# Causal masks added by VectorE instead of TensorE in a sparse-attention block, and ten early down-projection chunks instead of six

## The chip, the cores and the metric

The kernel runs on one core of a Trainium2 chip. The metric is the device time of one execution in microseconds (us), the median of several runs; lower is better. The core has five engines that run their own instruction queues in order: TensorE (PE; its weight loads are listed as PEld), VectorE (DVE), ScalarE (ACT), GpSimd (POOL) and SyncE (SP), which issues the DMAs. Matrix products are accumulated in PSUM; everything else on chip lies in SBUF.

## The reference

One decoder layer on x of 1024 tokens by 1024 channels, float32. RMSNorm and an input projection feed three groups of heads: pooling, native sparse attention and a short gated convolution. Their outputs go through w_out and are added to x; then comes a gated FFN of width 2816. The part that the change touches is the sparse attention, with 8 heads in 2 groups of 64 channels. Each head has three branches: compressed keys, selected blocks ("slc") and a sliding window of 512 ("win"). Cut to the two branches with full keys:

```
s_s = q . k_slc * scale - slope * d_s          # keys of the selected blocks
s_s = where(d_s >= 0, s_s, -1e30);  p_s = softmax(s_s);  o_s = p_s @ v_slc

ok  = (d_w >= 0) & (d_w < WINDOW)              # d = query position - key position
s_w = q . k_win * scale - slope * d_w
p_w = softmax(where(ok, s_w, -1e30));  o_w = p_w @ v_win

o = gate0 * o_cmp + gate1 * o_slc + gate2 * o_win
...
x = x + W_down( silu(causal_dwconv3(W_a h2)) * (W_b h2) )
```

## The kernel before

**Tiling.** Tokens are cut into 8 tiles of 128 queries. Products of float32 accuracy are made from a high and a low part of each operand (`split`, L86 to L89: ScalarE makes the high part, VectorE or GpSimd the low one), so one product is three matrix products. The program is written in the Tile framework: a planner decides, before the kernel runs, the order of the instructions on each engine, and puts in the semaphores. The order on an engine is then fixed.

**Attention.** `attend` (L639) walks over the tiles; for each it takes 2 groups and 2 branches (1 is the window, 0 the selected blocks), and weaves the scores of one unit (`scores`, L560) with the values of the unit before (`values`, L593). A row is one head of one unit: 128 queries against `ns` key tiles. `span` gives ns: the window branch takes at most 5 tiles of keys, the selected branch i + 1. With up to 4 key tiles a row is one chunk of columns, above that two. For each chunk, two products go to the PSUM tile S: L572 (the query's parts against the high key parts) and L573 (the query's high part, the slopes' rows and, for i >= 4, the selection's penalty, against the low key parts). The causal mask is added by a third product, L578, of a bfloat16 identity with `m_diag` (zeros and -2^100), into the last 128 columns of the row; in the window branch of tiles 4 to 7, L576 adds `m_edge` in the same way to the first 128 columns. Then VectorE takes the negative maximum of the row (L580), ScalarE the exp and its sum (L583), VectorE the reciprocal (L586), and GpSimd scales the row by it and the gate (L588). `values` transposes the row on TensorE (L97), splits it (`put_pt`, L472) and multiplies it with the values (L609, L610).

**Two attention stages.** Tiles 0 to 3 run first (L668), with two score buffers of one PSUM bank; the planner lays the convolution and pooling products beside them. Tiles 4 to 7 run second (L802), with one score buffer of two banks. Beside them lie the projection of the first four tiles (`project`), all 22 `up` products of the FFN for the first half of the tokens (their results go to DRAM as `hid0`), and then the early chunks.

**Early chunks.** The loop at L911 takes the first `EARLY` = 6 of 22 chunks of the down projection, two at a time, for tiles 0 to 3: it loads the hidden values (`hidden_in`, L874) and the down weights (`down_in`, L880), splits them, and adds the products (L925) to x2 on VectorE (L926). The memory of x2 is that of the up products' input, so this loop starts behind the last of these.

**FFN.** After the attention, `hidden_a` and `hidden_b` (L941, L950) go over the pairs of chunks in the order of `todo` (L980): first those that were not early, for which `down` (L955) also makes the products of tiles 0 to 3 (`first_half`, L983; two pairs ahead, the rest one per turn of the loop at L991), then the early ones, for which only tiles 4 to 7 are left. The down weights of every chunk are loaded and split here, also those of the early ones.

Of the kernel before, what the change touches and what calls it, by code (L numbers as in the profile page):

```python
# [10 lines left out]
BF16 = mybir.dt.bfloat16  # L11
I32 = mybir.dt.int32
AF = mybir.ActivationFunctionType
ALU = mybir.AluOpType
AX = mybir.AxisListType
# [3 lines left out]
P = 128  # L19
T = 1024  # L20
# [2 lines left out]
KT = D // P  # L23
DFF = 2816
NCH = DFF // P
EARLY = 6
DH = 64
EPS = 1e-6
NEG = -(2.0 ** 100)
# [16 lines left out]
def kernel(  # L46
# [7 lines left out]
    pe, dve, act, pool = nc.tensor, nc.vector, nc.scalar, nc.gpsimd  # L54
# [8 lines left out]
    cst = ctx.enter_context(tc.tile_pool(name="cst", bufs=1))  # L63
# [6 lines left out]
    def nm(s):  # L70
        uid[0] += 1
        return f"{s}_{uid[0]}"
# [242 lines left out]
    for s in range(2):  # L315
# [10 lines left out]
        bias = small(1, "cbias", 64)  # L326
# [34 lines left out]
    for c in range(2):  # L361
        wq = load_w(C_Q + 256 * c, (pool, dve))
        for i in range(NT):
# [6 lines left out]

    ident_b = cst.tile([P, P], BF16, name="ident_b")
    dve.tensor_copy(ident_b, ident)
    m_diag = cst.tile([P, P], BF16, name="m_diag")
    pool.memset(m_diag, 0.0)
    pool.affine_select(m_diag, m_diag, pattern=[[-1, P]], base=0, channel_multiplier=1,
                       compare_op=ALU.is_ge, fill=NEG)
    m_edge = cst.tile([P, P], BF16, name="m_edge")
    pool.memset(m_edge, 0.0)
    pool.affine_select(m_edge, m_edge, pattern=[[1, P]], base=-1, channel_multiplier=-1,
                       compare_op=ALU.is_ge, fill=NEG)  # L380
    m_cmp = cst.tile([P, NT, 64], BF16, name="m_cmp")
    pool.memset(m_cmp, 0.0)
    pool.affine_select(m_cmp, m_cmp, pattern=[[P, NT], [-16, 64]], base=-31, channel_multiplier=1,
# [94 lines left out]
        return hi, lo  # L478

    qAs, pcs, yfs, pos = {}, {}, {}, {}  # L480
    new_s, new_p = [None], [None]

    def prepare(i):

# [75 lines left out]
    def scores(i, g, br, pbs):  # L560

        s0, ns = span(i, br)
        nck = 1 if ns <= 4 else 2
        cw = ns * P // nck
        krows = 112 if (br == 0 and i >= 4) else 66
        for hh in range(4):
            S = new_s[0]()
            for c in range(nck):
                cols = slice(s0 * P + c * cw, s0 * P + (c + 1) * cw)
                last = c == nck - 1  # L570
                edge = br == 1 and i >= 4 and c == 0
                pe.matmul(S[:, c, :cw], qAs[i, g][:, hh, :], kA[br, g][:, cols], start=True, stop=False)  # L572
                pe.matmul(S[:, c, :cw], qB[g][i % QBUF][0:krows, hh, :], kB[br, g][0:krows, cols],  # L573
                          start=False, stop=not (last or edge))
                if edge:
                    pe.matmul(S[:, c, 0:P], ident_b, m_edge, start=False, stop=not last)  # L576
                if last:
                    pe.matmul(S[:, c, cw - P : cw], ident_b, m_diag, start=False, stop=True)  # L578
            mx = small(1, "mx1")
            dve.tensor_reduce(mx, S[:, 0:nck, :cw], axis=AX.XY, op=ALU.max, negate=True)  # L580
            pb = new_p[0](br)
            sw = small(1, "sw1")
            act.activation(pb[:, : ns * P].rearrange("p (c n) -> p c n", c=nck), S[:, 0:nck, :cw],  # L583
                           AF.Exp, bias=mx, accum_out=sw)
            rc = small(1, "rc1")
            dve.reciprocal(rc, sw)  # L586
            col = 8 * (2 if br == 1 else 1) + 4 * g + hh
            pool.tensor_scalar(pb[:, : ns * P], pb[:, : ns * P], rc, gat[:, i, col : col + 1],  # L588
                               ALU.mult, ALU.mult)
            pbs.append(pb)  # L590
            yield
# [203 lines left out]

    def f2k(dt=F32):
        return f2.tile([P, 512], dt, tag="f2k", bufs=5, name=nm("f2k"))

    sth = ExitStack()
    h2p = sth.enter_context(tc.tile_pool(name="h2a", bufs=1, side="right"))  # L800
# [224 lines left out]
```

## Time and profile before

| what | value |
|---|---|
| median of 3 runs | 1352.73 us (1352.63 to 1353.0) |
| profiled execution | 1353.7 us |
| its span, first to last instruction | 1351.9 us |
| mean granted TensorE clock | 0.995 |
| TensorE busy | 1313.2 us (97%) |
| VectorE busy | 765.6 us (57%) |
| ScalarE busy | 535.8 us (40%) |
| GpSimd busy | 495.1 us (37%) |

The profile is of one execution. The span is what the trace covers; the time of the execution is 1.8 us more. "Busy" counts an instruction from its start to its end; matrix products overlap in the array, so their listed duration is longer than the distance between two starts. Where a cost on TensorE is wanted, the distance between starts is to be read.

### The profile page before, as it was taken

The page shows a single profiled execution, that of the slowest core. Times are in us where ns is not written, and L with a number is a line of the kernel's source. Part 1 is how long each engine was busy: PE and PEld are TensorE (multiplying, and loading weights), DVE is VectorE, ACT ScalarE, POOL GpSimd, SP SyncE. Part 2 cuts the span into 40 slices and gives each one's busy share as a digit, 9 for nine tenths or more (in the row PEclk, how much of TensorE's full clock was granted, in tenths as well). Part 3 has the DMA queues.
Part 4 walks back from the last instruction along what each step waited for, and adds up shares of the span by engine and source line. Part 5 has one row for each costly group of instructions (what it writes and reads, how often), then busy time and mean ns, then how long its engine had stood idle before and what let it go on. Part 6 is the DMA issues. An engine that isn't in the chain of part 4 may idle for free. (4 is left out here: it accounts for less than half of the span.)

```text
span 1351.9 us, 17751 instructions
## 1 busy us (share of the span) xinstructions
PE 1313.2 (97%) x6670; PEld 1081.1 (80%) x6670; DVE 765.6 (57%) x1351; ACT 535.8 (40%) x972; POOL 495.1 (37%) x447
## 2 busy tenths in 40 slices
PE   6999999999998999999999999999999999999998
PEld 5999987678776788888888887778888788888886
DVE  6772556666776446445745667774454555454554
ACT  5441444444465444444544445453312322132220
POOL 3453723331334344434443545253313331242220
PEclk9999999999998999999999999999999999999999
DMA  9011320226342233222222273132222422243221
GB/s 274 16 48 56 102 58 20 86 97 220 125 149 94 78 101 94 86 79 86 87 78 78 86 251 100 48 110 71 84 62 78 125 63 78 79 156 92 84 74 62
DMA packets 142498, 128.93 MB, mean 95 GB/s; under 512 B 10595, under 2 KB 119373, under 8 KB 142413
## 3 DMA queue, kind: packets, MB, share of 16 engines
q1 hardware_dynamic: 142269, 127.71, 30.5%
q8 instruction: 52, 0.85, 0.3%
q14 instruction: 33, 0.27, 0.1%
q10 hardware_dynamic: 144, 0.10, 0.0%
HBM read 105.50 MB, written 22.28 MB: 95 GB/s over the span
## 5 line engine op out<-in xcount | busy, mean ns | idle before, releaser
L89 POOL TENSOR_TENSOR wlo<-wst,whi 128x1024 fp32r<-128x1024 f32 x109 | 264.3, 2438 | 281.5 <-ACT whi L88 273.6
L588 POOL TENSOR_SCALAR pb<-pb,rc,gat 128x640 f32<-128x640 f32 (+7 forms) x128 | 106.0, 829 | 317.8 <-DVE rc L586 302.0
L88 ACT ACTIVATE whi<-wst 128x1024 fp32r<-128x1024 f32 x124 | 127.1, 1056 | 125.7 <-DMA wst<-in_ffn_up_dram 80.1
L972 DVE TENSOR_TENSOR x<-dn,x 128x1024 f32<-128x1024 f32 x72 | 87.9, 1221 | 104.0 <-PE dn L969 104.0
L852 PE MATMUL fill<-h2a_hi,wlo 128*128 128x512 f32 x352 | 141.4, 402 | 0.0
L850 PE MATMUL fill<-h2a_hi,whi 128*128 128x512 f32 x352 | 141.3, 401 | 0.0
L851 PE MATMUL fill<-h2a_lo,whi 128*128 128x512 f32 x352 | 141.3, 401 | 0.0
L583 ACT ACTIVATE pb<-S,mx 128x640 f32<-128x640 f32 (+7 forms) x128 | 89.5, 700 | 114.6 <-DVE mx L580 108.4
L580 DVE TENSOR_REDUCE mx<-S 128x1 f32<-128x640 f32 (+7 forms) x128 | 89.6, 702 | 69.2 <-PE S L578 68.7
L477 DVE TENSOR_TENSOR ptl<-tr,pth 128x512 fp32r<-128x512 f32 x140 | 94.3, 685 | 54.7 <-PE acc L610 29.7
L476 ACT ACTIVATE pth<-tr 128x512 fp32r<-128x512 f32 x140 | 81.5, 595 | 80.4 <-PE tr L97 46.5
L969 PE MATMUL dn<-dl,hh 128*128 128x512 f32 x288 | 89.0, 390 | 0.0
L969 PE MATMUL dn<-dh,hl 128*128 128x512 f32 x288 | 88.6, 390 | 0.0
L969 PE MATMUL dn<-dh,hh 128*128 128x512 f32 x288 | 88.5, 391 | 0.0
L97 PE MATMUL tr<-ident,pb 128*128 128x128 f32 x528 | 83.4, 273 | 2.0 <-POOL pb L588 2.0
L857 DVE SCALAR_TENSOR_TENSOR f2k<-fill,colw,f2k 128x511 f32<-128x511 f32 x44 | 32.9, 749 | 86.0 <-ACT f2k L856 84.5
L850 PEld LDWEIGHTS fill<-h2a_hi,whi 128*128 128x128 f32 x352 | 66.3, 188 | 14.2 <-DVE h2a_lo L181 0.3
L851 PEld LDWEIGHTS fill<-h2a_lo,whi 128*128 128x128 f32 x352 | 66.4, 189 | 13.8
L852 PEld LDWEIGHTS fill<-h2a_hi,wlo 128*128 128x128 f32 x352 | 66.3, 188 | 13.6
L572 PE MATMUL S<-blk,qA 128*128 128x320 f32 (+5 forms) x192 | 70.1, 365 | 6.5 <-ACT pb L583 6.4
L97 PEld LDWEIGHTS tr<-ident,pb 128*128 128x128 f32 x528 | 64.4, 140 | 14.1 <-POOL pb L588 2.3
L856 ACT ACTIVATE f2k<-fill,colw 128x512 f32<-128x512 f32 x44 | 30.2, 686 | 110.2 <-PE fill L852 109.8
(275 smaller groups left out, 3173.0 us busy)
## 6 DMA issues: line engine op xcount, KB each, us to landing
wst<-in_ffn_up_dram SPq DMA_DIRECT2D x88, 512.0 KB, 3.9
wst<-in_ffn_down_dram SPq DMA_DIRECT2D x28, 512.0 KB, 3.7
wst<-in_w_in_dram SPq DMA_DIRECT2D x18, 512.0 KB, 4.6
wst<-in_w_out_dram SPq DMA_DIRECT2D x12, 512.0 KB, 4.5
hid<-f2k SPq DMA_DIRECT2D x22, 256.0 KB, 2.0
f2k<-hid SPq DMA_DIRECT2D x22, 256.0 KB, 3.6
b<-in_x_dram SPq DMA_DIRECT2D x8, 512.0 KB, 6.7
f<-in_x_dram SPq DMA_DIRECT2D x8, 512.0 KB, 4.9
```

The costliest lines, as they stand in the source:

```text
L88: act.activation(hi, src, AF.Copy)
L89: lo_eng.tensor_tensor(lo, src, hi.bitcast(F32), ALU.subtract)
L97: pe.transpose(out, src, ident[:n, :n])
L477: dve.tensor_tensor(lo, pt, hi.bitcast(F32), ALU.subtract)
L580: dve.tensor_reduce(mx, S[:, 0:nck, :cw], axis=AX.XY, op=ALU.max, negate=True)
L583: act.activation(pb[:, : ns * P].rearrange("p (c n) -> p c n", c=nck), S[:, 0:nck, :cw], AF.Exp, bias=mx, accum_out=sw)
L588: pool.tensor_scalar(pb[:, : ns * P], pb[:, : ns * P], rc, gat[:, i, col : col + 1], ALU.mult, ALU.mult)
L850: pe.matmul(ps, wh[:, kt, cols], h2[0][:, kt, :], start=kt == 0, stop=False)
L851: pe.matmul(ps, wh[:, kt, cols], h2[1][:, kt, :], start=False, stop=False)
L852: pe.matmul(ps, wl[:, kt, cols], h2[0][:, kt, :], start=False, stop=kt == KT - 1)
L969: pe.matmul(ps[:, nh - turn[0], :], h[:, tt], w[:, nh * 512 : nh * 512 + 512], start=k == 0 and h is hh and w is dh, stop=k == n - 1 and h ...
L972: dve.tensor_tensor(x2[:, i, ns], ps.rearrange("p a b -> p (a b)"), x2[:, i, ns], ALU.add)
```

## The change

Both mask products are taken out of `scores`. In their place stands one VectorE instruction per row, `tensor_tensor_reduce`, that adds a mask row to the scores, multiplies by -1, writes the result back to S and keeps its minimum, which is the negative maximum; it takes the place of the reduction at L580. The exp then reads S with scale -1. Two bfloat16 mask rows replace `m_diag` and `m_edge`: `m_win`, 640 columns with the edge in the first 128 and the diagonal in the last, of which shorter rows take the last columns; and `m_row`, 1024 columns with the diagonal in the last 128, for the selected branch of tiles 4 to 7, which is built when the second attention stage opens. Every row takes the new instruction over its whole width. `EARLY` goes from 6 to 10.

```diff
-EARLY = 6
+EARLY = 10
...
-    m_diag = cst.tile([P, P], BF16, name="m_diag")
-    pool.memset(m_diag, 0.0)
-    pool.affine_select(m_diag, m_diag, pattern=[[-1, P]], base=0, channel_multiplier=1,
+
+    m_win = cst.tile([P, 640], BF16, name="m_win")
+    pool.memset(m_win, 0.0)
+    pool.affine_select(m_win[:, 512:], m_win[:, 512:], pattern=[[-1, P]], base=0, channel_multiplier=1,
                        compare_op=ALU.is_ge, fill=NEG)
-    m_edge = cst.tile([P, P], BF16, name="m_edge")
-    pool.memset(m_edge, 0.0)
-    pool.affine_select(m_edge, m_edge, pattern=[[1, P]], base=-1, channel_multiplier=-1,
+    pool.affine_select(m_win[:, 0:P], m_win[:, 0:P], pattern=[[1, P]], base=-1, channel_multiplier=-1,
                        compare_op=ALU.is_ge, fill=NEG)
+
...
-                last = c == nck - 1
-                edge = br == 1 and i >= 4 and c == 0
                 pe.matmul(S[:, c, :cw], qAs[i, g][:, hh, :], kA[br, g][:, cols], start=True, stop=False)
                 pe.matmul(S[:, c, :cw], qB[g][i % QBUF][0:krows, hh, :], kB[br, g][0:krows, cols],
-                          start=False, stop=not (last or edge))
-                if edge:
-                    pe.matmul(S[:, c, 0:P], ident_b, m_edge, start=False, stop=not last)
-                if last:
-                    pe.matmul(S[:, c, cw - P : cw], ident_b, m_diag, start=False, stop=True)
+                          start=False, stop=True)
+
+            S = S[:, 0:nck, :cw]
+            m = (m_win if ns <= 5 and (ns <= 4 or br == 1) else m_row[0])
+            m = m[:, m.shape[-1] - ns * P :].rearrange("p (c n) -> p c n", c=nck)
             mx = small(1, "mx1")
-            dve.tensor_reduce(mx, S[:, 0:nck, :cw], axis=AX.XY, op=ALU.max, negate=True)
+            dve.tensor_tensor_reduce(S, S, m, scale=-1.0, scalar=3e38, op0=ALU.add, op1=ALU.min, accum_out=mx)
             pb = new_p[0](br)
             sw = small(1, "sw1")
-            act.activation(pb[:, : ns * P].rearrange("p (c n) -> p c n", c=nck), S[:, 0:nck, :cw],
-                           AF.Exp, bias=mx, accum_out=sw)
+            act.activation(pb[:, : ns * P].rearrange("p (c n) -> p c n", c=nck), S,
+                           AF.Exp, bias=mx, scale=-1.0, accum_out=sw)
...
+    m_row[0] = f2.tile([P, T], BF16, name="m_row")
+    pool.memset(m_row[0], 0.0)
+    pool.affine_select(m_row[0][:, T - P :], m_row[0][:, T - P :], pattern=[[-1, P]], base=0, channel_multiplier=1,
+                       compare_op=ALU.is_ge, fill=NEG)
```

## Rows read from the trace of the kernel before

**Rows 1.** The page's table of engines: busy us, share of the span, instructions.
```profile
PE 1313.2 (97%) x6670; PEld 1081.1 (80%) x6670; DVE 765.6 (57%) x1351; ACT 535.8 (40%) x972; POOL 495.1 (37%) x447
```

**Rows 2.** Busy time by stretch: from:to, length, PE, PEld, DVE, ACT, POOL, clock, DMA.
```profile
178.00:400.00 222.00, 213.78 (x1104) 169.32 (x1103) 147.22 (x298) 104.73 (x249) 71.41 (x90) 0.99 0.33 106
400.00:450.00 50.00, 42.78 (x224) 33.53 (x223) 31.34 (x73) 26.02 (x53) 20.09 (x17) 0.93 0.35 110
450.00:790.00 340.00, 340.00 (x1715) 276.61 (x1714) 185.08 (x359) 161.53 (x281) 147.53 (x94) 1.00 0.28 87
790.00:856.00 66.00, 65.30 (x335) 51.43 (x334) 44.93 (x70) 31.20 (x52) 30.31 (x22) 1.00 0.45 151
856.00:890.00 34.00, 31.54 (x141) 24.76 (x140) 24.55 (x33) 17.23 (x28) 11.28 (x9) 0.95 0.20 63
890.00:1352.00 462.00, 454.97 (x2000) 372.06 (x1998) 231.02 (x265) 120.57 (x152) 131.05 (x58) 1.00 0.29 88
```

**Rows 3.** TensorE's waits in 178:450 (first), 850:1352: total, times, longest us.
```profile
PE S L572 <- ACT pb L583: 6.4, 6, 1.9
...
PE upg L850 <- ACT whi L88: 2.7, 3, 1.1
PE fill L829 <- ACT yh L88: 2.2, 1, 2.2
```

**Rows 4.** Timeline of TensorE, a row with both masks: start, duration, instruction.
```profile
763.45 0.31 PE L573 MATMUL S<-blk,qB 66*128 66x320 f32 x1
763.60 0.23 PE L576 MATMUL S<-m_edge,ident_b 128*128 128x128 bf16 x1
763.64 0.39 PE L572 MATMUL S<-blk,qA 128*128 128x320 f32 x1
763.87 0.31 PE L573 MATMUL S<-blk,qB 66*128 66x320 f32 x1
764.02 0.23 PE L578 MATMUL S<-m_diag,ident_b 128*128 128x128 bf16 x1
...
764.38 0.39 PE L851 MATMUL fill<-h2a_lo,whi 128*128 128x512 f32 x1
764.60 0.39 PE L852 MATMUL fill<-h2a_hi,wlo 128*128 128x512 f32 x1
```

**Rows 5.** The same timeline, a row of five key tiles without edge product.
```profile
434.41 0.31 PE L573 MATMUL S<-blk,qB 112*128 112x320 f32 x1
...
434.70 0.31 PE L573 MATMUL S<-blk,qB 112*128 112x320 f32 x1
434.86 0.23 PE L578 MATMUL S<-m_diag,ident_b 128*128 128x128 bf16 x1
434.89 0.48 PE L610 MATMUL acc<-ptl,vv 128*128 128x512 f32 x1
435.21 0.60 PE L97 MATMUL tr<-ident,pb 128*128 128x128 f32 x4
```

**Rows 6.** VectorE's groups in 178:860 (L867: whole span), by shape: busy us, mean ns, idle.
```profile
L580 DVE TENSOR_REDUCE mx<-S 128x1 f32<-128x640 f32 x40 | 32.8, 819 | 28.1 <-PE S L578 27.8
L580 DVE TENSOR_REDUCE mx<-S 128x1 f32<-128x1024 f32 x8 | 9.8, 1219 | 2.7 <-PE S L578 2.7
L586 DVE RECIPROCAL rc<-sw 128x1 f32<-128x1 f32 x128 | 20.1, 159 | 38.3 <-ACT pb L583 36.3 <-POOL wlo L89 0.6
L926 DVE TENSOR_TENSOR x<-fill,x 128x512 f32<-128x512 f32 x24 | 16.4, 686 | 10.8 <-PE fill L925 9.8 <-DMA x<-xb 0.7
...
L867 DVE SCALAR_TENSOR_TENSOR f2k<-f2k,f2k 128x512 f32<-128x512 f32 x44 | 43.1, 981 | 26.2 <-ACT f2k L866 26.2
```

**Rows 7.** Diagonal products in one stretch (as rows 2); GpSimd's low halves, a group.
```profile
178.00:400.00 222.00, 14.79 (x64) 6.21 (x64) 0.99 0.33 106
...
L89 POOL TENSOR_TENSOR wlo<-wst,whi 128x1024 fp32r<-128x1024 f32 x109 | 264.3, 2438 | 281.5 <-ACT whi L88 273.6
```

More of the change, by code (lines that the diff above doesn't have):

```diff
@@ L480 @@
     qAs, pcs, yfs, pos = {}, {}, {}, {}
-    new_s, new_p = [None], [None]
+    new_s, new_p, m_row = [None], [None], [None]
     def prepare(i):
```

## The prediction

> **What bounds the kernel now.** First the page's table of engines: TensorE is busy 1313.2 of 1351.9 us, 97% [rows 1]. An average says nothing of where a cut pays, so the second view is busy time by stretch [rows 2], cut where the work changes: tiles 0 to 3 (178 to 400 us), the passage to tile 4 (400 to 450), tiles 4 to 7 beside the up products (450 to 790), the same beside the early down chunks (790 to 856), the attention's end (856 to 890) and the FFN (from 890). [...] From 450 to 856 TensorE idles 0.7 of 406 us at full clock: a product less there is time less. [...] From 856 to 890 it idles 2.5 us, and the clock (0.95) costs 1.7. The other engines have room everywhere: VectorE is busy 44.9 of 66 us in its fullest stretch. Third, TensorE's waits [rows 3]: in 178 to 450 the largest is a score product waiting for the exp of the row before (6.4 us); after 850 a projection waits 2.2 us for the last tile's attention output, and three up products wait for split weights (2.7 us). So TensorE's own order is the bound, with some 20 us of holes between 178 and 450 that the attention's chain makes.
>
> **What a mask product costs.** Its listed 0.23 us is pipelined and says little; I go by start to start. With the edge product, a tile's first qB product starts at 763.45 and its second at 763.87: 0.42 us [rows 4]. Without it the same pair, also of 320 columns, takes 434.41 to 434.70: 0.29 [rows 5]. So an edge product costs 0.13. A diagonal one: from its start to the second product behind it 0.36 (764.02 to 764.38) and 0.35 (434.86 to 435.21), where a plain 512-column step takes 0.22 to 0.23 (764.38 to 764.60) [rows 4, 5]: 0.13 again, of which 0.03 to 0.05 is its own step and the rest a late start of the product behind. Where the next product is as short as a transpose less of that delay should show, so I take 0.11 as the mean. There are 2 groups x 2 branches x 4 heads x 8 tiles = 128 diagonal products and, for the window branch of tiles 4 to 7, 32 edge ones: 128 x 0.11 + 32 x 0.13 = 14.1 + 4.2 = 18.3 us. The 64 diagonal ones of tiles 0 to 3 all lie in 178 to 400 [rows 7]: 7.0 us. The other 11.2 lie behind 400, nearly all of them where TensorE has no hole.
>
> [...]
>
> **What stays of it.** From 450 to 856 all, since nothing else is late there: a row of scores comes about every 7 us (56 rows in 406 us), while its own chain is a maximum of 0.8 to 1.2 us [rows 6] and an exp of about that. I take 10.5 of the 11.2. From 178 to 450 a chain that waits on VectorE, ScalarE and GpSimd doesn't get shorter by a product less; a hole can swallow the gain. I take two thirds, 4.7 of 7.0; the bounds are 0 and 7. Together **15.2 us**.
>
> **The new VectorE instruction.** Nothing in this trace adds, reduces and writes back to PSUM in one. From below: the reduction it replaces, 0.82 us at 640 columns, and the plain add of a PSUM and an SBUF operand, 0.69 at 512 [rows 6], which lies on the same line (the reductions rise by (1219 - 819) / 384 = 1.04 ns a column, so 0.69 at 512). From above: two full SBUF operands, 0.98 at 512 [rows 6], so 1.4 times. If the minimum leaves by an instruction of its own, that is at most another small one, 0.16 like the reciprocal [rows 6]. I take the reduction's time plus 0.16: the scores are a PSUM operand like the add's, which is the nearest row. That is 128 x 0.16 = 20 us more VectorE work, 766 to 786 of 1336 us, hidden as long as VectorE is short of its stretch. On a row's own chain it stands against the 0.12 of mask product that is gone: +0.04 a row. I set **+1.5 us** for it, about half of 72 rows up to 450; bounds -3 (the mask gone earlier from the chain) and the rival below. The exp with scale -1 is the same instruction. Behind the longer VectorE instruction are queued the reciprocals, the low halves of the transposed weights and the evictions; POOL's scaling of the row waits for the reciprocal.
>
> The mask rows cost GpSimd one wider fill before the first row, and a 1024-wide fill with one select before tile 4; it is busy 71 of 222 and 20 of 50 us there [rows 2], so 0, at most 1.
>
> **Ten early chunks.** Moved, not removed: 4 chunks x 4 tiles x 2 halves x 3 = 96 products of 0.23 = 22 us leave the FFN and go to the stretch before the last attention tile ends. What else goes with them: 4 hidden and 4 down-weight loads on SP's queue, 8 splits on ScalarE, 8 on GpSimd (down weights 2.44 us each [rows 7]), and 16 evictions of 0.69 [rows 6] on VectorE instead of 8 wide ones later. The down weights of these chunks are needed again for tiles 4 to 7, so their loads and splits are extra, beside a GpSimd at 30 of 66 us and a VectorE at 45 [rows 2]. A pair of chunks asks at most 4 x 2.44 = 9.8 us of GpSimd for 48 x 0.23 = 11 us of products, so it is covered; without that cover the pair would be late by what exceeds 11. The loads pass SP's queue ahead of the projections' inputs, which are due only after the last tile.
>
> What it gives: with 11 us less of TensorE work beside tiles 4 to 7 the filling would run out before the attention does; 22 us more keep TensorE fed. In the old order the filling ends as the attention does, and the last projection waits 2.2 us [rows 3] and drops the clock for 1.7 [rows 2]. With filling left this hole, 3.9 us, can close; next late would be the second norm of tiles 4 to 7, beside which the late chunks' products already lie. I take half, **-2.0**; bounds -3.9 and +2. In the FFN six turns with first-half products become four, and one of the three waits for split weights goes: 2.7 / 3 = **-0.9**; bounds -2.7 and +2.
>
> **The sum.** -15.2 + 1.5 - 2.0 - 0.9 = -16.6. The profiled execution took 1353.7 us (span 1351.9 and 1.8 around it): 1337.1. The median before, 1352.73, is 1.0 lower: **1336.1**. Its own range, with half of the holes' terms either way, is 1328 to 1344.
>
> **Rivals.**
> *Only the columns go.* The delay behind a mask product stays, because the score product now ends the group and its successor is as late. Then 160 x 0.04 = 6.4 us, 83% of it kept as above: -5.3 + 1.5 - 2.0 - 0.9 = -6.7, 1346.0. Against it: the pair without an edge product shows no delay [rows 5]. 0.08.
> *Waits take its place.* TensorE's order is fixed ahead of the run; where the chain of exp and transposes sets the pace, TensorE waits for what it no longer computes. All 7.0 of tiles 0 to 3 go that way, the hole at the end stays, and a passage to tile 4 that is drawn worse costs another 5: -11.2 + 1.5 + 5 = -4.7, 1348, and up to 1354. For it: 15 us of holes and the clock of 0.93 [rows 2]; against it: the solid 450 to 856. 0.13, of which 0.08 within 0.2%.
> *Slower: the instruction runs at half rate.* It reads the scores and the mask, writes the scores and keeps a minimum. At two steps a column, the 67,584 columns of the 128 rows cost 1.04 ns more each, 70 us, and the reading out 20: a row of tiles 0 to 3 is 0.49 us longer (31 us for 64 rows), one of tiles 4 to 7 0.9. The latter has room in 7 us. The former lies on the chain that TensorE waits for, with two score buffers: all exposed, 1336 + 31 = 1367; it makes the kernel slower once more than half (16.6 us) is exposed, so 1356 to 1367. Against it: the add at 0.69 with a PSUM operand runs at full rate [rows 6], and VectorE has 75 idle us in that stretch. 0.07.
> [...]
> *It doesn't do what it says*, the early chunks running only after the attention: the same products in another place, 0 from the move, inside the forecast's range.
>
> **Chances.** Forecast 0.72, columns 0.08, waits 0.13, slower 0.07. The range for 8 in 10 takes in the columns' case, most of the waits and a closing of all holes (18.3 + 3.9 + 2.7 + 2): 1326 to 1350. A measurement of this kernel tells 0.2% (2.7 us) from no change. Faster 0.72 + 0.08 + 0.05 = 0.85; same 0.08; slower 0.07.
>
> **What would show it.** No L576 and L578 products, and pairs of qB products 0.29 apart in every tile; the new instruction at 0.82 us for 640 columns, and 0.16 or less behind it; TensorE still without holes from 450 on and no more than 15 us of them before; 240 early products instead of 144, ending about with the attention; no wait of the last projection. I am wrong if the new instruction is over 1.2 us at 640 columns, if the holes from 178 to 450 grow by more than 10 us, or if the granted clock falls in a new stretch.

## The result, and the profile after

The kernel after takes **1340.92 us** (median; 1340.29 to 1341.26) against 1352.87 for the kernel before in the same comparison: ratio 0.9906, 95% interval 0.9892 to 0.992. The forecast was 1336.1, its own range 1328 to 1344. So 12.0 us are gained by the medians; by the two profiled executions, on which the accounts below rest, 13.0 (1353.7 to 1340.7).

The table of engines of the kernel after, as [rows 1]:

```profile
PE 1298.8 (97%) x6510; PEld 1081.2 (81%) x6510; DVE 764.2 (57%) x1487; ACT 541.9 (40%) x978; POOL 504.0 (38%) x452
```

160 matrix products are gone from 6670, and VectorE, which was to get 20 us more work, is busy no longer than before. Busy time by stretch, the columns as in [rows 2]:

```profile
178.00:400.00 222.00, 210.34 (x1030) 169.19 (x1029) 145.67 (x360) 103.19 (x246) 71.10 (x91) 0.98 0.33 106
400.00:450.00 50.00, 44.20 (x224) 35.66 (x225) 33.49 (x82) 26.51 (x54) 20.92 (x19) 0.90 0.35 111
450.00:790.00 340.00, 340.00 (x1684) 283.01 (x1682) 188.50 (x410) 166.25 (x283) 154.09 (x98) 1.00 0.32 99
790.00:856.00 66.00, 65.44 (x329) 53.75 (x328) 44.49 (x83) 31.77 (x54) 33.61 (x23) 1.00 0.36 116
856.00:890.00 34.00, 33.16 (x153) 26.31 (x152) 22.89 (x33) 15.20 (x25) 9.04 (x6) 1.00 0.30 93
890.00:1339.00 449.00, 442.32 (x1942) 361.32 (x1940) 231.47 (x265) 122.87 (x156) 131.22 (x59) 1.00 0.29 89
```

Three things are to be seen. From 450 to 856 TensorE idles 0.6 us at full clock, as before. From 856 to 890 the hole and the fall of the clock are gone. From 178 to 450 TensorE idles 11.7 + 5.8 us where it idled 8.2 + 7.2, and the mean granted clock is lower in both stretches.

TensorE's waits in the kernel after (total, times, longest us), in 178 to 450 and, behind the dots, in 850 to 1339; [rows 3] are those of before:

```profile
PE S L570 <- ACT pb L581: 11.2, 8, 2.2
PE fill L832 <- ACT yh L88: 1.4, 1, 1.4
...
PE upg L853 <- ACT whi L88: 0.9, 1, 0.9
PE fill L833 <- POOL wlo L89: 0.8, 1, 0.8
PE fill L97 <- DVE h2b_lo L181: 0.7, 1, 0.7
```

The wait of the last projection for the last tile's output (2.2 us) is gone, two of the three waits of up products for split weights are gone, and some short ones are new, one of them (0.8) of the last projection for its own split weights. In the first part the score products wait 11.2 us for the exp of the row before, not 6.4.

A row of the window branch on TensorE (start, duration, instruction), against [rows 4]:

```profile
760.16 0.31 PE L570 MATMUL S<-blk,qA 128*128 128x320 f32 x1
760.30 0.31 PE L571 MATMUL S<-blk,qB 66*128 66x320 f32 x1
760.45 0.31 PE L570 MATMUL S<-blk,qA 128*128 128x320 f32 x1
760.60 0.31 PE L571 MATMUL S<-blk,qB 66*128 66x320 f32 x1
760.75 0.40 PE L855 MATMUL fill<-h2a_hi,wlo 128*128 128x512 f32 x1
760.99 0.40 PE L853 MATMUL fill<-h2a_hi,whi 128*128 128x512 f32 x1
```

The two qB products start 0.30 us apart, where it was 0.42, and the next 512-column product starts without a delay. The new VectorE instruction (durations ns least/median/largest, first and last start us, shapes):

```profile
L578 DVE DVE_READ_ACCUMULATOR2_ANT mx<- x128: 82/141/145, 180.1 to 851.5; 128x1 f32 x128
L578 DVE CUSTOM_DVE_ANT_0 S<-S,m_row x32: 822/1028/1233, 433.1 to 850.3; 128x640 f32<-128x640 f32 x8, 128x768 f32<-128x768 f32 x8, 128x896 f32<-128x896 f32 x8, 128x1024 f32<-128x1024 f32 x8
```

It is two instructions: the pass over the row, on average 828 ns at 640 columns and 1228 at 1024, where the reduction took 819 and 1219 [rows 6], and the reading of the minimum, 141 ns. The reading starts before the listed end of the pass; from the start of the pass to the end of the reading all rows take 99 us, the reductions took 90. So a row is 0.07 us longer on VectorE.

**The account by stages.** The marks are the starts of four products on TensorE: the first score product, the first up product, the last up product of two high parts (`h2a_hi`, `whi`), and the last product of all. The first stage, between the first two marks, takes 263.1 us before and 261.1 after; the up stretch 349.5 and 337.7; the rest 557.1 and 556.5. These are 14.3 us less. The spans differ by 12.9, because the first score product starts 1.1 us later than before (at 179.4, not 178.3) and 0.3 us more lie behind the last product. What the mask products of each stage were worth follows from their count in the kernel before (stretch, length, busy us and number on TensorE, then PEld, clock, DMA; first the diagonal ones, then the edge ones):

```profile
178.00:441.30 263.30, 16.41 (x71) 6.89 (x71) 0.98 0.33 108
441.30:790.90 349.60, 10.61 (x46) 4.46 (x46) 1.00 0.28 87
790.90:1352.00 561.10, 2.54 (x11) 1.06 (x11) 1.00 0.30 94
...
178.00:441.30 263.30, 0.93 (x4) 0.39 (x4) 0.98 0.33 108
441.30:790.90 349.60, 5.53 (x24) 2.32 (x24) 1.00 0.28 87
790.90:1352.00 561.10, 0.93 (x4) 0.39 (x4) 1.00 0.30 94
```

At the prediction's 0.11 and 0.13 us these are 8.3, 8.2 and 1.7 us.

*The up stretch*, 8.2: it became 11.8 shorter. The difference is work that was put off: in it the kernel after has 258 transposes instead of 272, and 110 value products instead of 119. At some 0.1 us a transpose (an estimate: four in 0.60 listed [rows 5], and the next product starts 0.43 after the first) and 0.23 a 512-column product [rows 4] that is 3.5 us. One row of 1024 columns left it (0.9) and one of 640 came in (0.6). 8.2 + 3.5 + 0.3 = 12.0, against 11.8 seen. The price of a mask product is right.

*The first stage*, 8.3: it became 2.0 shorter. The same stretch of both kernels, before and then after:

```profile
178.00:441.00 263.00, 247.60 (x1282) 195.59 (x1281) 174.47 (x363) 128.34 (x296) 89.03 (x105) 0.98 0.33 108
```
```profile
178.00:441.00 263.00, 245.54 (x1209) 197.51 (x1208) 175.05 (x432) 126.28 (x292) 87.59 (x106) 0.96 0.33 107
```

TensorE idles 17.5 us instead of 15.4, 2.1 more. By the trace's clock records 20.4 us of the stretch lie at a granted clock of 0.50, instead of 10.2; half of that I count as lost, 10.2 instead of 5.1 us. (In the kernel after, from 425 to 427 us at 0.50, 512-column products start 0.43 us apart; behind 427.3, at 1.00, it is 0.23.) The row of 640 columns (four products, 0.6 us) and two transposes (0.2) are no longer in this stage. 8.3 - 2.1 - 5.1 + 0.8 = 1.9, against the 2.0 seen. Of these 2.0 only 1.2 are gained; 0.8 are put off.

*The rest*, 1.7: its holes fell from 6.5 to 4.2 us, and the 3.4 us at a clock of 0.50 at 883 us are gone (1.7 us). With the work put off into it this makes 1.7 - 3.5 - 0.9 + 2.3 + 1.7 = 1.3 us less; 0.5 are seen. Some 0.8 us of this stage I can't place.

### The profile page after: what moved, and what is told of

It reads as the page before. It is cut to its first block, busy times and chain, and to the rows that moved or that the text cites. A ratio compares the mean times of both kernels' runs of the same rounds, so it can differ in the third digit from the quotient of the medians.

```text
span 1339.0 us, 17613 instructions
## 1 busy us (share of the span) xinstructions
PE 1298.8 (97%) x6510; PEld 1081.2 (81%) x6510; DVE 764.2 (57%) x1487; ACT 541.9 (40%) x978; POOL 504.0 (38%) x452
## 4 chain that ended last, share of the span: by engine, by line
PE 89%; DVE 4%; DMA 3%; ACT 2%; issue 1%; POOL 0%; SPq 0%; ACTq 0%; DVEq 0%; POOLq 0%
PE dn L972 12%; PE fill L853 9%; PE fill L855 9%; PE fill L854 9%; PE tr L97 4%; PE fill L928 4%; PE upg L853 3%; PE upg L855 3%; PE upg L854 3%; PE S L570 2%; PE fill L211 2%; PE S L571 2%; PE fill L212 2%; PE fill L213 2%; PE acc L608 2%; PE acc L607 2%
## 5 line engine op out<-in xcount | busy, mean ns | idle before, releaser
L89 POOL TENSOR_TENSOR wlo<-wst,whi 128x1024 fp32r<-128x1024 f32 x113 | 273.5, 2434 | 305.4 <-ACT whi L88 305.2
L88 ACT ACTIVATE whi<-wst 128x1024 fp32r<-128x1024 f32 x128 | 131.1, 1055 | 136.0 <-DMA wst<-in_ffn_up_dram 80.7
L975 DVE TENSOR_TENSOR x<-dn,x 128x1024 f32<-128x1024 f32 x64 | 78.2, 1221 | 89.0 <-PE dn L972 88.8
L578 DVE CUSTOM_DVE_ANT_0 S<-S,m_win 128x640 f32<-128x640 f32 (+4 forms) x96 | 57.7, 607 | 41.4 <-PE S L571 40.9
L972 PE MATMUL dn<-dh,hh 128*128 128x512 f32 x256 | 79.1, 391 | 0.5 <-DVE x L975 0.5
L972 PE MATMUL dn<-dh,hl 128*128 128x512 f32 x256 | 79.2, 391 | 0.0
L972 PE MATMUL dn<-dl,hh 128*128 128x512 f32 x256 | 79.0, 390 | 0.0
L570 PE MATMUL S<-blk,qA 128*128 128x320 f32 (+5 forms) x192 | 67.0, 352 | 11.2 <-ACT pb L581 11.2
L854 PEld LDWEIGHTS fill<-h2a_lo,whi 128*128 128x128 f32 x352 | 66.3, 188 | 13.5
L853 PE MATMUL upg<-h2b_hi,whi 128*128 128x512 f32 x176 | 69.1, 393 | 1.0 <-ACT whi L88 0.9
```

Of the source, the lines that this page charges most:

```text
L88: act.activation(hi, src, AF.Copy)
L89: lo_eng.tensor_tensor(lo, src, hi.bitcast(F32), ALU.subtract)
L853: pe.matmul(ps, wh[:, kt, cols], h2[0][:, kt, :], start=kt == 0, stop=False)
L854: pe.matmul(ps, wh[:, kt, cols], h2[1][:, kt, :], start=False, stop=False)
L972: pe.matmul(ps[:, nh - turn[0], :], h[:, tt], w[:, nh * 512 : nh * 512 + 512], start=k == 0 and h is hh and w is dh, stop=k == n - 1 and h ...
```

## The experiments

Theory A is the prediction's working. The rivals in the expectations: B, that another order drawn by the planner makes the difference and not the work; C, that the new instruction and its read-out take back part of the gain; D, that in tiles 4 to 7 a row's own chain sets the pace of the attention and is hidden only as long as TensorE has other work. Medians are in us, ratios are to the kernel before in the same comparison.

**1. The masks alone.** The kernel after with six early chunks.

```diff
-EARLY = 10
+EARLY = 6
```

> The mask change alone: the kernel after with six early chunks. Theory A (saturation: a mask product is worth its 0.13 us only where TensorE has no hole, from 440 us on; the early chunks fill the attention's end): the stretch of up products keeps its gain of about 12 us, but the filling runs out before the attention, so the hole before the last projection is as before (2.2 us and a drop of the clock) or larger: 1343 to 1350. Rival B (the order that the planner draws decides, not the amount of work): within 2 us of the kernel after, or below it, with the holes in other places.

1343.73, ratio 0.9927 (0.9913 to 0.9942). The hole before the last projection is back:

```profile
PE fill L832 <- ACT yh L88: 2.2, 1, 2.2
PE upg L853 <- ACT whi L88: 2.0, 2, 1.1
```

The last early product starts at 840 us, the last value product at 870; with ten chunks it is 875 and 872. So with the masks off TensorE the four added chunks are worth 2.8 us by the medians, close to the 2.0 + 0.9 set for them; the two intervals just overlap.

**2. The early chunks alone.** The kernel before with ten.

```diff
-EARLY = 6
+EARLY = 10
```

> The early chunks alone: the kernel before with ten early chunks. Theory A: only the hole before the last projection closes and one wait in the FFN goes, 2 to 5 us: 1348 to 1351; the stretch from 178 to 441 us and the up products as before. Rival B: any change of up to 10 us either way.

1352.04, 0.9996 (0.9987 to 1.0006): no change that can be told, where 2 to 5 us were expected. The hole before the last projection is gone here too, but two waits of 0.9 and 1.0 us are new behind 850. The profile shows where the gain went. The rest, from the last up product on, is 553.4 us, against 557.1 in the kernel before and 555.6 in its second profile (run 12). Ahead of that, up to 839 us, TensorE's products stand in the same order as in the kernel before, and yet the first up product starts at 443.0 us, against 441.3 and 442.4: from 178 to 441 there are 17.1 us at a clock of 0.50 instead of 10.2. So the chunks do give something with the masks on, and it is not shown that they need the masks off. With the masks off the filling would end 30 us ahead of the attention, not 24; that this makes the chunks worth more is a guess.

**3 and 4. The masks of one half of the tiles.** The mask products stay on TensorE for tiles 0 to 3 (run 3), or for tiles 4 to 7 (run 4), with the reduction for these rows.

```diff
+                on_pe = i < 4          # run 4: i >= 4
...
+                if last:
+                    pe.matmul(S[:, c, cw - P : cw], ident_b, m_diag, start=False, stop=True)
...
+            if on_pe:
+                dve.tensor_reduce(mx, S, axis=AX.XY, op=ALU.max, negate=True)
+            else:
+                dve.tensor_tensor_reduce(S, S, m, scale=-1.0, scalar=3e38, op0=ALU.add, op1=ALU.min, accum_out=mx)
...
```

> The kernel after with the mask products back in tiles 0 to 3 (64 diagonal products on TensorE, plain reduction on VectorE); tiles 4 to 7 by the new instruction. Theory A: the holes from 178 to 440 us swallow these products, so no change: 1341, within 2 us. Theory C (the reading of the accumulator, 0.14 us a row, lengthens the chain that TensorE waits for there): 1336 to 1339, as the 64 rows lose it. If the products were worth their price there too: 1346 to 1348.

> The reverse: the new instruction in tiles 0 to 3 alone, mask products (64 diagonal, 32 edge) in tiles 4 to 7, ten early chunks. Theory A: the gain of the up products' stretch goes: 1341 + 11 = 1352 (1349 to 1353). If the gain came from the early chunks or from tiles 0 to 3: 1343 or less.

Run 3: 1343.39, 0.9927 (0.9912 to 0.9941). The 64 products of tiles 0 to 3, 7.0 us by their price, cost 2.5, a little more than the 2 that A allowed. Run 4: 1349.14, 0.9969 (0.9958 to 0.9981). The 96 products of tiles 4 to 7 cost 8.2 of 11.2. The up stretch is 337.7 us long in run 3, as in the kernel after, and 350.5 in run 4: what is won there is won by the products of tiles 4 to 7, by A. The 8.2 as a whole is no clean price. Tiles 0 to 3 are masked in run 4 as in the kernel after, but the planner drew them in another order, and the first up product starts 2.5 us earlier (437.9 against 440.4).

**5. Twice the masks.** The kernel before with each mask product of tiles 4 to 7 issued twice (one mask more in an already masked place changes no probability).

```diff
                 if edge:
+                    pe.matmul(S[:, c, 0:P], ident_b, m_edge, start=False, stop=False)
...
+                    if i >= 4:
+                        pe.matmul(S[:, c, cw - P : cw], ident_b, m_diag, start=False, stop=False)
```

> The price of a mask product by adding: the kernel before, with each mask product of tiles 4 to 7 issued twice (64 diagonal and 32 edge ones more; the mask is twice as low, the softmax is the same). Theory A with the price read from the rows (0.13 edge, 0.11 diagonal): +11.2, 1364. By own steps alone, 0.04 each: +4, 1357. A second product of the same weights behind the first may cost less than the first, since the late start of the product behind is paid once: then +4 to +6 and the price of the first isn't refuted.

1357.02, 1.0031 (1.0017 to 1.0046): 96 products more cost 4.2 us, 0.044 each and not 0.12. The planner drew another order from 410 us on. In the up stretch alone, which is 6.9 us longer, 72 products were added; without the score, value and transpose products that also came in (2.1 to 2.4 us), that is 0.06 to 0.07 each. TensorE's timeline of one row:

```profile
769.11 0.23 PE L576 MATMUL S<-m_edge,ident_b 128*128 128x128 bf16 x1
769.18 0.22 PE L577 MATMUL S<-m_edge,ident_b 128*128 128x128 bf16 x1
769.21 0.39 PE L572 MATMUL S<-blk,qA 128*128 128x320 f32 x1
769.44 0.31 PE L573 MATMUL S<-blk,qB 66*128 66x320 f32 x1
769.59 0.23 PE L580 MATMUL S<-m_diag,ident_b 128*128 128x128 bf16 x1
769.65 0.22 PE L581 MATMUL S<-m_diag,ident_b 128*128 128x128 bf16 x1
769.68 0.47 PE L855 MATMUL fill<-h2a_hi,wlo 128*128 128x512 f32 x1
769.99 0.39 PE L853 MATMUL fill<-h2a_hi,whi 128*128 128x512 f32 x1
```

From the first diagonal product to the second product behind the pair there are now 0.40 us (769.59 to 769.99), against 0.36 with one [rows 4]. The second product adds 0.04 here and 0.06 for the edge pair; the late start of the product behind is paid once a group. That is the split that the prediction read (0.03 to 0.05 its own step, the rest the delay), and why taking the whole group away pays 0.11 to 0.13 where adding a second pays 0.04. The second one's price here, 0.04 to 0.07, is about half of the first one's or less.

**6. No masks at all.** The masks are left out altogether; reduction and exp are those of the kernel before, ten early chunks.

```diff
-            dve.tensor_tensor_reduce(S, S, m, scale=-1.0, scalar=3e38, op0=ALU.add, op1=ALU.min, accum_out=mx)
+            dve.tensor_reduce(mx, S, axis=AX.XY, op=ALU.max, negate=True)
...
-                           AF.Exp, bias=mx, scale=-1.0, accum_out=sw)
+                           AF.Exp, bias=mx, accum_out=sw)
```

> The kernel after with no mask added at all (neither products nor the new instruction; the old reduction and exp; the softmax then also covers the keys ahead of the query and behind the window), ten early chunks. Shows what is left when the products go for nothing. Theory A (178 to 440 us swallows its share by holes of the chain and the clock, whatever VectorE does): 1341 within 2 us. Theory C (the reading of the accumulator takes the gain of tiles 0 to 3 back): 1335 to 1338.

1341.46, 0.9914 (0.99 to 0.9929): the same as the kernel after, as A expected. C, which wanted 3 to 6 us less, falls. The +1.5 of the sum can't be told from nothing by these medians. The lower clock and the holes of the first stage are there without it too:

```profile
178.00:441.00 263.00, 245.68 (x1213) 198.13 (x1212) 172.93 (x363) 127.22 (x295) 88.70 (x107) 0.96 0.33 107
```

**7. A longer chain of the row.** Between the new instruction and the exp stands one more reduction over the row (some 90 us of VectorE in all, 0.3 to 1.2 per row).

```diff
-            dve.tensor_tensor_reduce(S, S, m, scale=-1.0, scalar=3e38, op0=ALU.add, op1=ALU.min, accum_out=mx)
+            mx2 = small(1, "mx2")
+            dve.tensor_tensor_reduce(S, S, m, scale=-1.0, scalar=3e38, op0=ALU.add, op1=ALU.min, accum_out=mx2)
+            dve.tensor_reduce(mx, S, axis=AX.XY, op=ALU.min)
```

> The slower rival by a stand-in: the kernel after with one more VectorE reduction on each row's chain, between the new instruction and the exp (0.29 to 1.22 us a row, 90 us of VectorE work; it takes the minimum again from the scores written back). Theory A: hidden in tiles 4 to 7, half exposed in tiles 0 to 3 (64 rows, 31 us): 1341 + 15 = 1356 (1349 to 1364). If VectorE had room everywhere: 1343 or less. If it were the bound near 800 us too: 1370 and more.

**1387.19**, 1.0249 (1.0226 to 1.0272): 46 us more than the kernel after, three times what I expected. The profiled execution took 1382.5, 42 more than that of the kernel after: 10 of these lie before the first up product (450.3 us, not 440.4). Its stretches behind that:

```profile
600.00:790.00 190.00, 190.00 (x924) 157.35 (x923) 114.20 (x223) 85.43 (x143) 86.83 (x52) 1.00 0.37 118
790.00:870.00 80.00, 76.99 (x381) 62.30 (x380) 66.13 (x130) 38.67 (x69) 40.26 (x28) 1.00 0.31 100
870.00:945.00 75.00, 58.10 (x261) 43.57 (x260) 52.16 (x81) 34.05 (x59) 20.37 (x17) 0.91 0.11 36
```

From 600 to 790 TensorE is full, as the prediction's slower rival says. But between 450 and 780 the rows come every 8.4 us instead of 7.4, so the last score product starts at 916 instead of 850, while the early chunks end at 869. From 870 on nothing is left to hide the chain: 17 us of holes at a clock of 0.91.

Why do the rows come further apart? Here is a row of 768 columns beside the up products, in the kernel after and then in run 7 (start, duration, instruction, and in brackets ScalarE's idle time before it): its first score product, its exp, and the first score product of the next row.

```profile
566.07 0.34 PE L570 MATMUL S<-blk,qA 128*128 128x384 f32 x1
...
568.03 0.90 ACT L581 ACTIVATE pb<-S,mx 128x768 f32<-128x768 f32 x1
...
573.01 0.31 PE L570 MATMUL S<-blk,qA 128*128 128x320 f32 x1
```
```profile
609.76 0.34 PE L570 MATMUL S<-blk,qA 128*128 128x384 f32 x1
...
612.77 0.91 ACT L583 ACTIVATE pb<-S,mx 128x768 f32<-128x768 f32 x1 [2.86 <-DVE mx L580]
...
618.49 0.31 PE L570 MATMUL S<-blk,qA 128*128 128x320 f32 x1
```

In the kernel after the exp has left the score buffer at 568.93, and the next row begins 4.1 us later; in run 7 it is 4.8 us. By the median of the rows from 450 to 780, a row holds the buffer for 3.0 us in the kernel after and 4.4 in run 7, and the buffer then stands free for 4.3 us in both. So it isn't the exp as it runs that holds the next row back there. The next row begins where it stands in TensorE's order, and the planner drew that order with the rows 1.0 us further apart. Why it leaves this distance isn't shown. Behind 870 it is otherwise: the buffer is free for 0.6 us by the median, and TensorE waits for the scaled rows (5.0 us), the split transposes (4.4) and the exp (3.2).

**8. Another order.** The second mask row is filled by VectorE instead of GpSimd; the planner puts 306 lines of TensorE's order elsewhere; in the two traces the products differ between 293 and 400 us.

```diff
-    pool.memset(m_row[0], 0.0)
+    dve.memset(m_row[0], 0.0)
```

> The kernel after with the 1024-wide fill of the second mask row moved from GpSimd to VectorE: no work of weight changes, but the planner draws 306 lines of TensorE's order differently. Rival B (the order drawn decides): a change of several us. Theory A: within 1.5 us of the kernel after.

1341.63, 0.992 (0.9903 to 0.9937): 0.7 us by the medians, so this reordering changes nothing that can be told. For the up stretch B falls: it is 337.7 us in the kernel after and in runs 1, 3, 6, 8 and 10, and 349.5 in both profiles of the kernel before and in run 2. For the first stage one reordering is little evidence; in run 4 another order reached the first up product 2.5 us earlier.

**9. More filling at tile 4.** The first holes of the passage are scores that wait for the exp. Here is the kernel after (start, duration, instruction, and in brackets the idle time before it and who ended it):

```profile
416.64 0.46 PE L570 MATMUL S<-blk,qA 128*128 128x320 f32 x1 [2.18 <-ACT pb L581]
...
419.81 0.63 PE L570 MATMUL S<-blk,qA 128*128 128x320 f32 x1 [1.90 <-ACT pb L581]
```

Run 9 moves the projection of tokens 4 to 7 behind the second norm, so that more work than before stays for the time beside the attention; its weights are loaded and split again.

```diff
-    for i in range(NT):
+    for i in range(4):
...
+    ws = load_wout((0, 6), (pool, pool))
+    for i in range(4, NT):
...
```

> The kernel after with the first projection of tokens 4 to 7 (96 products, 22 us of TensorE work that waits for nothing of the attention) moved behind the second norm in the program, so that it can lie in the passage from tile 3 to tile 4; its weights are loaded and split a second time. Tests that the holes and the half clock between 384 and 427 us (10 us of lower clock, about 8 us of waits) keep the products' gain of tiles 0 to 3: if so, 5 us less, 1336 (1333 to 1339). If the passage is held by the chain from tile 3's values to the second norm alone, and tile 3 gets no earlier by less filling: 1341 or up to 5 more.

1352.81, 0.9995 (0.9985 to 1.0005): 12 us lost, more than either expectation allowed. The waits of scores for the exp fell (6.8 us from 178 to 456, against 11.2 up to 450), but the 20.4 us at a clock of 0.50 stayed. The attention ended 18 us earlier (last value product 854), but the first up product came 15 us later (456), and the filling ended alone, with a new hole of 3 us and a clock of 0.94:

```profile
PE fill L932 <- DVE x L933: 4.1, 4, 3.1
...
860.00:890.00 30.00, 25.29 (x99) 18.85 (x97) 16.90 (x20) 6.32 (x8) 11.26 (x6) 0.94 0.36 115
```

The guess that the passage only lacked filling isn't borne out; how much of the loss belongs to the weights that are loaded and split again isn't known.

**10. Fourteen early chunks.**

```diff
-EARLY = 10
+EARLY = 14
```

> The kernel after with 14 early chunks. Theory A: filling beyond the attention's end changes nothing: 1341 within 1.5 us (in the kernel after the last early product starts at 874.6 and the last value product at 871.8).

1346.78, 0.9946 (0.9931 to 0.9961): 5 to 6 us more, where I expected none. The early chunks now run 32 us beyond the attention's end (last one at 904, last value product at 872), and there they are late themselves. TensorE's waits behind 860, and the place (ACT and PEld left out):

```profile
PE fill L928 <- DVE x L929: 4.0, 4, 3.1
...
889.94 2.36 POOL L89 TENSOR_TENSOR wlo<-wst,whi 128x1024 fp32r<-128x1024 f32 x1
890.04 3.33 DVE L89 TENSOR_TENSOR wlo<-wst,whi 128x1024 fp32r<-128x1024 f32 x1 [1.74 <-POOL yl L89]
...
893.30 1.28 DVE L929 TENSOR_TENSOR x<-fill,x 128x512 f32<-128x512 f32 x2
...
894.03 0.50 PE L928 MATMUL fill<-whi,yh 128*128 128x512 f32 x1 [3.08 <-DVE x L929]
```

A weight split of the projection stands in VectorE's queue ahead of the eviction that frees the accumulator, and TensorE waits 3.1 us for it. Holes and clock make 4.7 of the 5.8 us between the two profiles: 3.0 us more of holes behind the last up product, and 1.7 at a stretch with a clock of 0.50 at 895 us that the kernel after doesn't have.

**11. The longer chain with eighteen chunks.** Run 7 with EARLY = 18, to tell D from a mere cost of the added instructions.

> The kernel with the longer row chain (1387) with 18 early chunks. Theory D (in tiles 4 to 7 the chain of a row sets the attention's pace, one score buffer; a longer chain costs nothing as long as there is filling, and all of it once the filling is out): 8 chunks or 45 us more of filling close the holes behind 868, 25 to 35 us less: 1352 to 1362. If VectorE itself is the bound there: 1383 or more.

1362.87, 1.0069 (1.0052 to 1.0085): 24 us of the 46 come back with the longer chain still in place, a little less than the 25 to 35 that D set. The stretch that had 17 us of holes:

```profile
870.00:945.00 75.00, 74.40 (x364) 60.40 (x364) 57.26 (x97) 37.69 (x61) 38.02 (x25) 1.00 0.29 88
```

The last score product starts at 916 in both, though from 870 on TensorE has 16 us more of work here. So where the attention ends does not depend here on how much other work TensorE has beside it, and what a late end costs depends on how long that work lasts. VectorE isn't the bound: it does more in this stretch than in run 7 (57.3 us against 52.2), and the rows come no later. That much of D holds. That the chain sets the pace as it runs is shown only behind 870 in run 7; before that the rows stand where the planner put them. Of the 22 us that remain, 12.5 lie before the first up product (452.9).

**12. The kernel before once more**, unchanged, for the clock of its first stage.

> The kernel before, unchanged, profiled once more. In the kernel after and in three kernels with the same first stage (early six, no masks, fourteen early chunks) the trace has half clock at 263 (3.4 us), 293 (6.8) and 417 (10.2): 20.4 us between 178 and 441, so the places recur. The trace of before has 10.2 us there, the kernel before with ten early chunks 17.1. Theory K (the lower clock of tiles 0 to 3 belongs to the order of the products and recurs with it): 10.2 us again, at 269 and 419, and the change really pays 5 us of clock there. Theory L (the first profile of before caught an execution with less of it): 15 us or more at half clock here. Time by both 1352.7 within 1.

1353.22, 1.0003 (0.9994 to 1.0013), and 13.6 us at a clock of 0.50 from 178 to 441: between K and L. One place is new and two recur. In the kernel after, and with its masks removed, with six and with fourteen chunks, it is 20.4 us each time, in the same places; in run 2 it is 17.1. Run 2 belongs here too, since its products stand in the order of the kernel before up to 839 us. So one and the same order had 10.2, 13.6 and 17.1 us at a clock of 0.50 in three executions. The new order's 20.4 is more than any of them, by 3.3 to 10.2 us, 1.7 to 5.1 us of time; the first profile of the kernel before lies at one end of that. Its holes from 178 to 441 are 15.4, 14.2 and 13.0 us, against 16.9 to 17.6 in the kernel after and runs 1 and 10. Why the new order loses more clock isn't settled: run 6 has it without the new instruction, and run 3, with the products back in tiles 0 to 3, again 20.4.

## Why the prediction was right, and where its sum was off

**What bounds the kernel: right.** TensorE without holes from 450 on turns products into time. The up stretch gives it within 0.2 us (8.2 of masks and 3.8 put off, against 11.8), runs 3 and 4 give it by tiles. Of the 20 us of holes between 178 and 450, 15.4 are idle time; the other 5 are the lower clock, 10.2 us at 0.50.

**The price of a mask product: right,** 0.11 to 0.13 with the delay of the product behind. The rival "only the columns go" (0.04 each, 1346) falls: the delay went with the group, as the pair without an edge product [rows 5] had shown. Its price is the one that run 5 measured for a product *added* to a group.

**What stays in tiles 0 to 3: mis-sized.** Two thirds, 4.7 of 7.0 us, were kept; run 3 gives 2.5. The account by stages gives 1.2 of 8.3 for the whole first stage, and 1.2 to 3.4 if three profiles with each order are taken (before, runs 2 and 12; after, runs 1 and 10). The reason named ("a hole can swallow the gain") is what the rows show: 2.1 us more of holes, in which the scores' waits for the exp grew by 4.8 (6.4 to 11.2 [rows 3]) while others fell, and 1.7 to 5.1 us of lower clock, which the sum had at nothing. The profile's 178 to 450, with 15 us of holes and a clock below 1 [rows 2], was a reason to keep a third. Of the signs named, one failed: 17.5 us of holes from 178 to 450, not at most 15. None of the three conditions of being wrong was met: the holes grew by 2, and the clock fell further in two stretches of [rows 2] that were below full clock already.

**What stays in tiles 4 to 7: all of it in the up stretch; the 10.5 as a whole is not settled.** By the account by stages the products beside the up stretch gave everything, 8.2 us. 7 diagonal and 4 edge ones of tile 4 lie ahead of it in the passage, in a stage that gave little, and 15 behind the last up product (1.7 us), where 0.8 us can't be placed. Run 4's 8.2 for all 96 products holds an order that is 2.5 us faster ahead of them.

**The new instruction: nothing that can be told, where +1.5 was set.** It runs at the reduction's rate, 1.04 ns a column as that does, and with its reading a row takes 0.07 us longer, not 0.16. The rival "half rate" doesn't occur. The nearest row, the plain add, was right. The bound from above was misread: the 0.98 us of two SBUF operands [rows 6] is a mean of two kinds. In the trace of the kernel before 34 of these 44 instructions take 0.67 to 0.69 us, the add's time, and ten take 0.89 to 2.48, each of which started under a GpSimd instruction and ended 0.54 to 0.55 us behind its end (last section). So with two float32 operands from SBUF the 34 are no slower than the add with one in PSUM (0.67 to 0.69).

**But the price of that rival was wrong.** It gave a longer row chain 15 to 31 us, all in tiles 0 to 3, since a row of tiles 4 to 7 "has room in 7 us". Run 7, with a chain longer by 0.3 to 1.2 us a row, lost 10 us before the first up product, where 15 were expected, and the larger part behind the last one. The room was read rightly: the score buffer stands free for 4.3 of 7.4 us. What failed is the step from room to no cost. It took TensorE's order as given, but the planner draws it anew, and with a longer chain it put the rows further apart; the last score product then started 66 us later, when the filling was out. It did no harm only because the new instruction was fast.

**The early chunks: right in size with the masks off** (2.8 for the 2.9 set). With the masks on the medians show nothing (run 2), though the rest was 2 to 4 us shorter there; whether the two parts hang together isn't settled. The limit was not seen: four more cost 5 to 6 us (run 10), because beyond the attention's end an early product waits for a VectorE that the projection has taken.

**Waits take their place** (1348, chance 0.13) happened in part: up to the first up product more holes and a lower clock took 5 to 7 of 8.3 us, but the hole at the end did close. The runs taken one by one give 2.5 + 8.2 + 2.8 = 13.5 us, the change as a whole 12.0; each of the three is uncertain by a microsecond or two, so the difference says nothing. Of the 4.6 us that the sum had too much, 2.2 are those of tiles 0 to 3 by run 3; the rest isn't told apart.

No kernel of this study that computes the masks beats the kernel after; run 8 equals it at 1341.6, and runs 1 and 10, with fewer and more early chunks, take 1343.7 and 1346.8.

## What to carry to other kernels

Price a small instruction from start to start, with the delay of its successor, and take it at full value only in stretches where TensorE neither idles nor loses clock; where it idled for another engine's chain, about a third or less was kept here. Before calling a longer chain hidden, ask how the planner will space its rows, and not only whether there is room in the order that it drew before; then ask whether the work that hides the chain lasts to its end. Of 6, 10 and 14 chunks the best was the amount that ended with the attention.

## What the runs showed of the hardware

Two things were new to me. A short product between 512-column products cost 0.04 to 0.07 us itself here and 0.06 to 0.09 as a late start of the next, once for the group (run 5).

And many VectorE instructions with two operands in SBUF ended late when they had started under a GpSimd instruction. The weight split took 3.33 us in run 10, where nine of the 15 of this shape in the kernel after take 1.21 to 1.30. In the rows above GpSimd's split starts 0.1 us ahead of it and ends at 892.30; VectorE's ends 1.07 us later. This is no single case. The rows of the kernel before hold the ten slow ones of L867; here is one (start, duration, instruction):

```profile
968.79 2.40 POOL L89 TENSOR_TENSOR wlo<-wst,whi 128x1024 fp32r<-128x1024 f32 x1 [24.81 <-ACT whi L88]
969.26 2.48 DVE L867 SCALAR_TENSOR_TENSOR f2k<-f2k,f2k 128x512 f32<-128x512 f32 x1 [1.71 <-ACT f2k L866]
```

GpSimd's split ends at 971.19, VectorE's instruction 0.55 us later; it took 2.48 us, where 34 of the 44 take 0.67 to 0.69. All ten started under a GpSimd instruction and ended 0.54 to 0.55 us behind its end, however long it had still to run; the slow weight splits of the kernels before and after and of run 10 end 1.07 to 1.09 us behind one. The new instruction, with one operand in PSUM, took 0.82 to 0.83 us in all its 40 rows of 640 columns, 16 of which started under a GpSimd instruction. It isn't so each time: an L867 at 528.37 us started under a GpSimd scaling that had 1.28 us to run, and took 0.69. Why the late ones are late isn't shown.
